# Paged decode inside a hybrid decoder step: value pages multiplied in runs of four, with ten page buffers and an 8 KB transfer scratch

## The chip, the cores and the metric

The kernel runs on one core of a Trainium2 chip. Its time is the device time of one execution in microseconds (us); the figure for a kernel is the median of several executions.

## The reference, cut to what matters

One inference step of a two-layer decoder: a gated-linear-attention (GLA) layer, then a differential-attention layer, each followed by a squared-ReLU MLP. There is a prompt of 1024 tokens (with 16 meta tokens before it), and eight running sequences that each get one new token. For those eight, the second layer attends over 4096 past tokens, held as 32 pages of 128 tokens in a pool:

```python
def diff_sample(x, cache_k, cache_v, page_table, w_in, lam, lam_init, g_sub, w_out):
    ...
    k_past = cache_k[page_table].reshape(B, past, DIFF_HEADS, 2, DIFF_DH)
    v_past = cache_v[page_table].reshape(B, past, DIFF_HEADS, DIFF_DV)
    k_all = jnp.concatenate([k_past, k], axis=1)
    v_all = jnp.concatenate([v_past, v], axis=1)
    o = diff_core(q, k_all, v_all, pos, jnp.arange(past + T), lam)

def diff_core(q, k, v, q_pos, k_pos, lam):
    s = jnp.einsum('bqhmd,bkhmd->bhmqk', q, k) * (DIFF_DH ** -0.5)
    p = jax.nn.softmax(jnp.where(mask, s, -jnp.inf), axis=-1)
    a = p[:, :, 0] - lam * p[:, :, 1]
    return jnp.einsum('bhqk,bkhe->bqhe', a, v)
```

A key page and a value page are each 128 x 1024 float32, 512 KB. Eight sequences of 32 pages make 256 key pages and 256 value pages, and each sequence has one more value row, that of its new token.

## The kernel before, in words

The large products (projections and MLPs of the prompt) run on TensorE as three float32r products of a split into a high and a low part (`mm3`, lines 185 to 188). The stages follow each other: GLA (up to some 520 us), then its output projection and the first MLP, then the projection of the second layer (`L1049` on), then prompt attention (from 1787 us), then its output projection and the second MLP.

The paged decode of the eight sequences is a generator, `decode()` (line 848), that runs beside the first MLP and the second layer's projection. Its step for sequence b handles, page by page, the keys of sequence b and the values of sequence b-1:

- `k_page` (line 783) loads a key page into a buffer of the pool `pgp` (line 726, `PGB` buffers of 4 KB per partition), multiplies it by the broadcast query (line 789, on VectorE, every fourth page on GpSimd) and sums it to scores (line 790, VectorE). Then its buffer is free.
- `v_load` (line 816) loads a value page into a buffer of the same pool. The buffer is held until TensorE has multiplied the page.
- `v_pages` (line 825) multiplies the value pages that are held: per page four products with 16 stationary columns each, in four column strips of the array, into one accumulator `acc` (line 830). They are plain float32, which the trace shows as two instructions each, so a page is eight matmul records.
- `soft` (line 792) is the softmax at the start of a sequence's values. Its transposes and sums pass through TensorE (lines 797, 801 and 806).
- `v_end` (line 836) takes the accumulator out after the 33rd value page (line 822 loads the new token's row).

All page loads are issued on SyncE's queue in `page` (lines 753 to 759). The sequences are numbered b = 0 to 8: b = 0 has keys alone, b = 8 values alone.

The order of instructions on each engine is fixed when the kernel is built, by a scheduler that plans with a timeline (`schedule_with_timeline_sim=True`). Page loads and key work stand in the background (`background()`, line 730): they have the lowest priority. The products of `v_pages` are not in the background; they stand at the priority of the place where the generator was advanced, ahead of most of the first MLP. The first product of a run is tied behind the reduction of a key page (`behind`, line 831), which fixes its place in the order:

```python
                    if len(held) == 2:
                        v_pages(held, w, acc, k)
                        held = []
                    held.append((n, v_load(b - 1, n)))
            if b > 0:
                held.append((NPG, v_load(b - 1, NPG)))
                v_pages(held, w, acc, None)
```

At the end of a sequence, and in b = 8, there is no such tie (`None`). The pages with numbers in `HOLD` (32 b + n from 212 to 227) are spread over the steps of the second layer's projection.

TensorE multiplies with the whole 128 x 128 array in `mm3`, and with strips of 16 columns in `v_pages`. A run here is a stretch of TensorE's order in which only products of line 830 follow each other.

GpSimd issues its own transfers (accumulating weight loads at line 1414, copies at lines 1149 to 1156 and 1378 to 1393). The scratch that the program reserves for such transfers is 16 KB per partition by default.

Of the kernel before, what the change touches and what calls it, by code (L numbers as in the profile page):

```python
# [32 lines left out]
EPS = 1e-5  # L33
NEG = -1e30
LAM_INIT = 0.8 - 0.6 * math.exp(-0.3)
PGB = 8
HOLD = range(212, 228)
HTB = 1
LEVELS = (64, 32, 16, 8, 4, 2, 1)
# [71 lines left out]
def hybrid_step(ctx, tc, A, dbg=None, upto=9):  # L111
    nc = tc.nc
# [19 lines left out]
    def smt():  # L132
        return sm.tile([P, 512], F32, name="smt")
# [591 lines left out]
    dp2 = de.enter_context(tc.tile_pool(name="dp2", bufs=2))  # L725
    pgp = de.enter_context(tc.tile_pool(name="pgp", bufs=PGB))
    bg_at = [10 ** 7]
# [46 lines left out]
    def k_start(b):  # L774
        sc = dp2.tile([P, NPG + 1, 16], F32, name="sc")
        qb = dp.tile([P, D], F32, name="qb")
        with background():
            dma(qb, A["qs"][b : b + 1, :].broadcast_to([P, D]))
            V.memset(sc[:, NPG, :], NEG)
            V.tensor_scalar(sc[:NS, NPG, :], own, other[:NS, b : b + 1], None, ALU.add)  # L780
        return sc, qb

    def k_page(b, n, sc, qb):
        with background():
            pg = page("cache_k", b, n)
            eng, after = (G, steps_g) if n % 4 == 3 else (V, steps_v)

            with tc.issue_after(after[-1]) if (b == 0 and n < 24 and after) or HOLD.start <= NPG * b + n < NPG * (HOLD.start // NPG + 1) else nullcontext():
                eng.tensor_tensor(pg, pg, qb, op=ALU.mult)  # L789
            return V.tensor_reduce(sc[:, n, :], pg.rearrange("p (h d) -> p h d", d=64), op=ALU.add, axis=AX.X).ins  # L790

    def soft(sc):

        mx = dp.tile([P, 16], F32, name="mx")
        V.tensor_reduce(mx, sc.rearrange("p n c -> p c n"), op=ALU.max, axis=AX.X)
        ps = smt()
        TE.transpose(ps[:16, :P], mx, ident)
        m1 = dp.tile([16, 1], F32, name="m1")
        V.tensor_reduce(m1, ps[:16, :P], op=ALU.max, axis=AX.X)
        ps = smt()  # L800
        TE.matmul(ps[:, :16], m1.broadcast_to([16, P]), ident[:16, :16], start=True, stop=True)
        V.tensor_tensor(sc, sc, bc(ps[:, :16], [P, NPG + 1, 16], 1), op=ALU.subtract)
        S.activation(sc, sc, AF.Exp, scale=0.125)
        V.tensor_reduce(mx, sc.rearrange("p n c -> p c n"), op=ALU.add, axis=AX.X)
        ps = smt()
        TE.matmul(ps[:, :16], one, mx, start=True, stop=True)
        cf = dp.tile([P, 16], F32, name="cf")
        V.reciprocal(cf, ps[:, :16])
        cv = cf.rearrange("p (c m) -> p c m", m=2)
        V.tensor_tensor(cv, cv, bc(lamv, [P, 8, 2], 1), op=ALU.mult)  # L810
        V.tensor_tensor(sc, sc, bc(cf, [P, NPG + 1, 16], 1), op=ALU.mult)
        av = sc.rearrange("p n (c m) -> p n c m", m=2)
        V.tensor_tensor(av[:, :, :, 0], av[:, :, :, 0], av[:, :, :, 1], op=ALU.add)
        return sc

    def v_load(b, n):
        with background():
            if n < NPG:
                return page("cache_v", b, n)
            pg = pgp.tile([P, D], F32, name="pg")  # L820
            G.memset(pg[:32], 0.0)
            dma(pg[:NS], A["v_rows_s"][0, :, 0].rearrange("b h d -> b (h d)"))
            return pg

    def v_pages(pages, w, acc, behind):

        for n, pg in pages:
            r = slice(0, P if n < NPG else 32)
            for i in range(4):
                m = TE.matmul(acc[i * TS : i * TS + 16, :256], w[r, n, :], pg[r, i * 256 : (i + 1) * 256], start=n == 0, stop=n == NPG).ins  # L830
                if behind is not None:

                    tc.add_manual_dep(m, behind.name, mybir.DependencyInfo(mybir.DependencyClass.NoSync, mybir.DependencyReason.DATA), reason="order")
                    behind = None

    def v_end(b, acc):

        ev = pgp.tile([P, D], F32, name="pg")[:, :256]
        G.memset(ev, 0.0)
        for i in range(4):  # L840
            S.copy(ev[i * TS : i * TS + 16, :], acc[i * TS : i * TS + 16, :256])
        pt = smt()
        for j in range(2):
            TE.transpose(pt[:, j * P : (j + 1) * P], ev[:, j * P : (j + 1) * P], ident)
        for j in range(2):
            V.tensor_copy(oT[:, j : 8 : 2, b], pt[:, 130 * j : 130 * j + 36 * 3 + 1 : 36])

    def decode():
        ks = None
        for b in range(NS + 1):  # L850
            prev = ks
            if b < NS:
                ks = k_start(b)
            if b > 0:
                w = soft(prev[0])
                acc = smt()
            held, k = [], None
            for n in range(NPG):
                if b == 0 or NPG * b + n in HOLD:
                    yield b  # L860
                if b < NS:
                    k = k_page(b, n, *ks)
                if b > 0:

                    if len(held) == 2:
                        v_pages(held, w, acc, k)
                        held = []
                    held.append((n, v_load(b - 1, n)))
# [3 lines that stand above are left out]
                v_end(b - 1, acc)  # L872
# [155 lines left out]
    for u in range(4):  # L1028
        dma(Yt[:, :, u * 256 : (u + 1) * 256], A["x_prompt"][0, :, u * 256 : (u + 1) * 256].rearrange("(t p) n -> p t n", p=P))
    stats = ln_stats(hp)  # L1030
    paged = decode()
    normalize(w_out(A["gla_w_out"][0], False, paged), stats, lambda c: to_fm(c, 0))
    normalize(mlp(paged), stats, lambda c: to_fm(c, 1))
# [538 lines left out]
```

## Time and profile before

| | |
|---|---|
| Median of 3 runs | 2902.23 us (2901.81 to 2903.02) |
| Profiled execution, its own time | 2897.76 us |
| Span of its trace | 2896.0 us |
| Granted TensorE clock, mean | 0.981 |
| TensorE busy | 2773.3 us (96%) |
| VectorE, ScalarE, GpSimd busy | 1882.9, 1043.5, 1132.4 us |
| Moved by DMA | 636.46 MB, mean 220 GB/s |

In the profile, PE is TensorE's matmul, PEld its weight load, DVE VectorE, ACT ScalarE, POOL GpSimd, SP SyncE; a q behind a name is the engine's queue of issues. L830 is line 830 of the kernel. A row of instructions has the start and the duration in us, the engine, the line, the operation, out<-in, the shapes and the count of merged records. Matmuls are pipelined and their ends are modelled, so the pace is read from their starts. A row of waits has who waited for whom, the total in us, how often, and the longest.

### The profile page before, as it was taken

The numbers are of one execution on the slowest core, as the hardware profiler recorded it, in microseconds if no ns is written. First come the engines' busy times: TensorE is split into PE (matmuls) and PEld (weight loads), VectorE is DVE, ScalarE is ACT, GpSimd is POOL, SyncE is SP. The second block draws the span as 40 slices with busy tenths as digits, with TensorE's granted clock in tenths as the row PEclk, the third lists the DMA queues.
The fourth block names the chain that finished last, engine by engine and source line by source line (L and its number), as shares of the span: only waits on it lengthen the run. The fifth ranks groups of instructions, "written<-read, shape, count | busy, mean of one in ns | idle before, by whom it ended". The sixth has DMA issues, their size and how long they took to land. (4 is left out here: it accounts for less than half of the span.)

```text
span 2896.0 us, 52075 instructions
## 1 busy us (share of the span) xinstructions
PE 2773.3 (96%) x19653; PEld 2267.4 (78%) x19653; DVE 1882.9 (65%) x2982; ACT 1043.5 (36%) x2075; POOL 1132.4 (39%) x867
## 2 busy tenths in 40 slices
PE   8889999999999999999999999989998999999997
PEld 5666767997777777777798988888988888797985
DVE  2565544567878777778768822888538846738378
ACT  3233444252221221221231112777424535345352
POOL 1231212234333433333333321122426766777664
PEclk9899999999999999999999998999999999999998
DMA  7557651624798898898668995463447678695894
GB/s 250 181 176 261 245 177 39 231 73 145 268 350 299 301 351 303 321 323 310 254 225 302 363 341 142 101 137 82 120 132 220 174 220 222 160 287 119 258 240 88
DMA packets 285366, 636.46 MB, mean 220 GB/s; under 512 B 25510, under 2 KB 141292, under 8 KB 273852
## 3 DMA queue, kind: packets, MB, share of 16 engines
q1 hardware_dynamic: 252716, 520.66, 52.4%
q0 software_dynamic: 32400, 112.50, 16.2%
q8 instruction: 154, 2.52, 0.4%
q14 instruction: 96, 0.79, 0.1%
HBM read 575.55 MB, written 44.06 MB: 214 GB/s over the span
## 5 line engine op out<-in xcount | busy, mean ns | idle before, releaser
L174 POOL TENSOR_TENSOR wlo<-raw,whi 128x512 fp32r<-128x512 f32 x256 | 357.1, 1408 | 730.1 <-ACT whi L173 635.8
L186 PE MATMUL mmt<-whi,XH 128*128 128x256 f32 (+1 forms) x1760 | 526.1, 300 | 2.2 <-ACT Y L310 2.0
L187 PE MATMUL mmt<-wlo,XH 128*128 128x256 f32 (+1 forms) x1760 | 525.9, 299 | 0.9 <-POOL wlo L174 0.9
L186 PE MATMUL mmt<-XH,whi 128*128 128x512 f32 (+1 forms) x1216 | 436.5, 360 | 7.0 <-DVE HL L183 6.6
L188 PE MATMUL mmt<-whi,XL 128*128 128x256 f32 x1536 | 436.6, 285 | 0.5 <-DVE XL L183 0.5
L188 PE MATMUL mmt<-XH,wlo 128*128 128x512 f32 (+1 forms) x1216 | 434.3, 358 | 0.0
L173 ACT CAST whi<-raw 128x512 fp32r<-128x512 f32 x256 | 153.1, 619 | 579.5 <-PE mmt L188 206.3
L187 PEld LDWEIGHTS mmt<-wlo,XH 128*128 128x128 f32 x1760 | 332.2, 189 | 30.9 <-issue 19.0
L186 PEld LDWEIGHTS mmt<-whi,XH 128*128 128x128 f32 x1760 | 331.5, 189 | 28.2 <-issue 13.5
L790 DVE TENSOR_REDUCE sc<-pg 128x16 f32<-128x1024 f32 x256 | 309.5, 1214 | 62.5 <-POOL pg L789 59.3
L187 PE MATMUL mmt<-XL,whi 128*128 128x512 f32 x768 | 307.3, 400 | 0.0
L188 PEld LDWEIGHTS mmt<-whi,XL 128*128 128x128 f32 x1536 | 289.8, 189 | 13.5 <-issue 11.8
L789 DVE TENSOR_TENSOR pg<-pg,qb 128x1024 f32<-128x1024 f32 x192 | 263.7, 1375 | 53.4 <-DMA pg<-in_cache_k 38.2
L789 POOL TENSOR_TENSOR pg<-pg,qb 128x1024 f32<-128x1024 f32 x64 | 158.8, 2482 | 297.9 <-DMA pg<-in_cache_k 182.4
L186 PEld LDWEIGHTS mmt<-XH,whi 128*128 128x128 f32 x1216 | 230.6, 190 | 54.8 <-issue 14.6
L188 PEld LDWEIGHTS mmt<-XH,wlo 128*128 128x128 f32 x1216 | 231.0, 190 | 38.1 <-issue 5.9
L187 PE MATMUL mmt<-wlo,HH 128*128 128x512 f32 x512 | 204.7, 400 | 0.0
L188 PE MATMUL mmt<-whi,HL 128*128 128x512 f32 x512 | 204.6, 400 | 0.0
L186 PE MATMUL mmt<-whi,HH 128*128 128x512 f32 x512 | 204.4, 399 | 0.0
L187 PEld LDWEIGHTS mmt<-XL,whi 128*128 128x128 f32 x768 | 145.5, 190 | 38.3 <-issue 7.1
L1416 POOL TENSOR_TENSOR wlo<-RW,whi 128x512 fp32r<-128x512 f32 x96 | 156.7, 1762 | 37.1 <-ACT whi L1415 37.1
L1416 POOL TENSOR_TENSOR wlo<-rw,whi 128x512 fp32r<-128x512 f32 x92 | 148.8, 1690 | 43.3 <-ACT whi L1415 43.2
(441 smaller groups left out, 5745.6 us busy)
## 6 DMA issues: line engine op xcount, KB each, us to landing
pg<-in_cache_k SPq DMA_DIRECT2D x256, 512.0 KB
pg<-in_cache_v SPq DMA_DIRECT2D x256, 512.0 KB
XH<-xc POOLq DMA_DIRECT2D x42, 1032.0 KB, 8.7
raw<-in_mlp_w SPq DMA_DIRECT2D x164, 256.0 KB
swt<-in_mlp_w SPq DMA_DIRECT2D x32, 1024.0 KB
rw<-in_mlp_w SPq DMA_DIRECT2D x116, 256.0 KB
RW<-in_mlp_w POOLq DMA_DIRECT2D x96, 256.0 KB, 6.1
xc<-XH POOLq DMA_DIRECT2D x14, 1032.0 KB, 7.6
```

The costliest lines, as they stand in the source:

```text
L173: S.copy(hi[:, c], raw)
L174: G.tensor_tensor(lo[:, c], raw, hi[:, c].bitcast(F32), op=ALU.subtract)
L186: TE.matmul(ps, ah, bh, start=first, stop=False)
L187: TE.matmul(ps, ah, bl, start=False, stop=False)
L188: TE.matmul(ps, al, bh, start=False, stop=last)
L789: eng.tensor_tensor(pg, pg, qb, op=ALU.mult)
L790: return V.tensor_reduce(sc[:, n, :], pg.rearrange("p (h d) -> p h d", d=64), op=ALU.add, axis=AX.X).ins
L1416: G.tensor_tensor(lo[:, k, :], t, hi[:, k, :].bitcast(F32), op=ALU.subtract)
```

## The change

Three numbers change. `v_pages` is called when four value pages are held, not two. The pool of page buffers has ten buffers, not eight. The scratch for GpSimd's transfers is 8 KB per partition, not 16; the two page buffers need 8 KB per partition.

```diff
-PGB = 8
+PGB = 10
+RUN = 4
...
-                    if len(held) == 2:
+                    if len(held) == RUN:
                         v_pages(held, w, acc, k)
                         held = []
...
-    nc = bacc.Bacc("TRN2", target_bir_lowering=False, num_devices=1)
+    nc = bacc.Bacc("TRN2", target_bir_lowering=False, num_devices=1, dynamic_dma_scratch_size=8192)
```

Per sequence, `v_pages` is called with fifteen groups of two pages and one of three before, and with seven groups of four and one of five after.

## The prediction

> **What bounds the kernel now.** I read the page first, then the busy time by stretches, the waits of TensorE, and the timeline around single runs of value pages.
>
> ```profile
> span 2896.0 us, 52075 instructions
> PE 2773.3 (96%) x19653; PEld 2267.4 (78%) x19653; DVE 1882.9 (65%) x2982; ACT 1043.5 (36%) x2075; POOL 1132.4 (39%) x867
> PE   8889999999999999999999999989998999999997
> DMA  7557651624798898898668995463447678695894
> ```
>
> TensorE is busy 96% of the span, and the slices from the eleventh to the twenty-fourth, where the pages are read, show it at nine tenths nearly throughout, with the DMA engines at six to nine tenths. Busy time of a pipelined engine proves little, so the next view cuts out the stretch from the first run of value pages to the end of the second layer's projection, and the third asks what TensorE waits for in it.
>
> ```profile
> core 0: us, PE busy (x) PEld busy (x) DVE busy (x) ACT busy (x) POOL busy (x), PEclk, DMA share, GB/s
> 520.00:766.00 246.00, 238.51 (x1404) 209.02 (x1402) 172.11 (x203) 74.00 (x122) 85.92 (x54) 0.98 0.51 169
> 766.00:1787.00 1021.00, 1019.55 (x7006) 795.71 (x7005) 703.18 (x831) 233.40 (x408) 348.67 (x222) 1.00 0.84 302
> ```
> ```profile
> PE smt L801 <- DVE m L799: 1.0, 1, 1.0
> PEld smt L830 <- DMA pg<-in_cache_v: 4.8, 13, 0.4
> ```
>
> In 1021 us TensorE is idle for 1.45 us, at full granted clock (1.00). The longest wait of its matmuls is one of 1.0 us, in a softmax; the weight loads of page products waited for a landing 13 times, 0.4 us at most, and these waits lie beside matmuls. DVE is busy 703 of 1021 us, the DMA engines 0.84 of the time. So this stretch is bound by TensorE's own sequence of instructions: a microsecond taken out of that sequence is a microsecond off the end, as long as pages, softmax and weights keep up.
>
> **What a run costs.** The timeline of TensorE around three runs of two, six and four pages (16, 48 and 32 records):
>
> ```profile
> 905.91 0.39 PE L187 MATMUL mmt<-wlo,HH 128*128 128x512 f32 x1
> 906.14 0.40 PE L188 MATMUL mmt<-whi,HL 128*128 128x512 f32 x1
> 906.46 1.06 PE L830 MATMUL smt<-pg,sc 128*16 128x256 f32 x16
> 907.45 0.50 PE L186 MATMUL mmt<-whi,HH 128*128 128x512 f32 x1
> 907.79 0.40 PE L187 MATMUL mmt<-wlo,HH 128*128 128x512 f32 x1
> ```
> ```profile
> 1010.45 0.40 PE L188 MATMUL mmt<-whi,HL 128*128 128x512 f32 x1
> 1010.78 2.78 PE L830 MATMUL smt<-pg,sc 128*16 128x256 f32 x48
> 1013.49 0.51 PE L186 MATMUL mmt<-whi,HH 128*128 128x512 f32 x1
> 1013.83 0.39 PE L187 MATMUL mmt<-wlo,HH 128*128 128x512 f32 x1
> ```
> ```profile
> 1562.95 0.28 PE L188 MATMUL mmt<-whi,XL 128*128 128x256 f32 x1
> 1563.16 1.92 PE L830 MATMUL smt<-pg,sc 128*16 128x256 f32 x32
> 1565.01 0.39 PE L186 MATMUL mmt<-whi,XH 128*128 128x256 f32 x1
> 1565.24 0.28 PE L187 MATMUL mmt<-wlo,XH 128*128 128x256 f32 x1
> 1565.36 0.28 PE L188 MATMUL mmt<-whi,XL 128*128 128x256 f32 x1
> ```
>
> The starts are what counts. Ordinary 512-column products start 0.23 us apart (905.91 to 906.14), 256-column ones 0.12 us (1565.24 to 1565.36). From the last ordinary product before a run to the second one after it there are two ordinary starts and the run: 907.79 - 906.14 = 1.65, less 2 x 0.23, leaves 1.19 us for two pages; 1013.83 - 1010.45 = 3.38, less 0.46, leaves 2.92 us for six; 1565.24 - 1562.95 = 2.29, less 0.24, leaves 2.05 us for four. From two to six pages that is 1.73 / 4 = 0.43 us a page, and what is left of a run, however long, is 1.19 - 2 x 0.43 = 0.33 us (2.05 - 4 x 0.43 = 0.33 for four pages). I use 0.32 us: the price of leaving the ordinary products and coming back. The change removes no page product; it removes such prices.
>
> [...]
>
> **How many prices go.** The products of line 830 in the whole trace, then the runs of one sequence (first two and last two of 13), then of the last sequence (two of its 27):
>
> ```profile
> L830 PE MATMUL smt<-pg,sc 128*16 128x256 f32 (+1 forms) x2112 | 139.0, 382 | 0.0
> ```
> ```profile
> 1133.15 2.78 PE L830 MATMUL smt<-pg,sc 128*16 128x256 f32 x48
> 1143.69 1.06 PE L830 MATMUL smt<-pg,sc 128*16 128x256 f32 x16
> ...
> 1215.35 1.06 PE L830 MATMUL smt<-pg,sc 128*16 128x256 f32 x16
> 1222.38 2.47 PE L830 MATMUL smt<-pg,sc 128*16 128x256 f32 x40
> ```
> ```profile
> 1697.00 0.62 PE L830 MATMUL smt<-pg,sc 128*16 128x256 f32 x8
> ...
> 1751.89 1.18 PE L830 MATMUL smt<-pg,sc 128*16 128x256 f32 x16
> ```
>
> 2112 records are 264 pages, eight sequences of 33. The sequence shown has six pages at once after its softmax, eleven runs of two, and five pages at its end: 13 runs out of 16 calls of `v_pages`, because the first three groups and the last two are ready together. Counted so on the timeline, the sequences b = 1 to 6 have 81 runs (13 or 14 each), b = 7 has 17 (three single pages at its end), and b = 8 has 27, nearly all single pages, because nothing ties them behind a key page: 125 runs in all, whose prices are 125 x 0.32 = 40 us. No merging can save more.
>
> After the change there are eight calls a sequence. At the start two groups of four may be ready together (one run fewer); at the end the group of five has no tie and may fall into two or three pieces (one or two more). I take 8 runs for b = 1 to 6 (48 for 81, 33 fewer), 9 for b = 7 (8 fewer), and 25 for b = 8, where ten buffers let more pages wait for the softmax (2 fewer): 43 fewer, 43 x 0.32 = 13.8 us. From below: if each end splits into three further pieces, 24 fewer, 7.7 us. From above: 7 runs in each of b = 1 to 7 and 22 in b = 8 make 71 runs, 54 fewer, 17.3 us. I take 13.8, since the sequence shown merges at both ends.
>
> **What the other parts cost.** Held pages. The loads wait for buffers already now:
>
> ```profile
> SPq L758 <- DVE sc L790: 102.4, 87, 4.0
> SPq L758 <- PE smt L830: 84.8, 73, 5.7
> ```
>
> SyncE's issues waited for a buffer from a key reduction 87 times and from a page product 73 times, and TensorE still had no idle time, so these waits are covered. Just before a run, two value pages and the key page under reduction hold three of eight buffers now, and four and one hold five of ten after: five are left for loads in both. A run will give back four at once instead of two, half as often. That cover is equal at its tightest, so I cost it at nothing; without it, a page takes 0.524 MB / 302 GB/s = 1.7 us to come in at this stretch's rate. In sequence b = 0 two more key pages can be fetched early: at most 2 x 1.7 = 3.5 us of transfer ahead of the weights, in a stretch (520 to 766 us) with the DMA engines at 0.51 and TensorE idle 7.5 us. Its bounds are a loss of 3.5 and a gain of 7.5 us; I take nothing, because with keys alone no page is held.
>
> What is late next, when TensorE gains 14 us? The last run ends near 1753 us and the accumulator is out soon after, while the projection goes on to 1787:
>
> ```profile
> 1757.08 0.23 DVE L846 COPY oT<-smt 128x4 f32<-128x4 f32 x2 [28.21 <-PE smt L844]
> 1787.18 0.27 PE L188 MATMUL mmt<-whi,XL 128*128 128x256 f32 x1
> ```
>
> That leaves 30 us, so the decode's own end doesn't take over.
>
> The scratch. GpSimd's transfers are those of q0:
>
> ```profile
> q0 software_dynamic: 32400, 112.50, 16.2%
> RW<-in_mlp_w POOLq DMA_DIRECT2D x96, 256.0 KB, 6.1
> ```
>
> None lies in the decode, and no row shows an issue that waits for scratch. I cost it at nothing; the other end is below. [...]
>
> The sum: 2897.8 us of the profiled execution (1.8 us around the span) less 13.8 makes 2884.0. The median of the runs is 4.5 us above the profiled execution, so the forecast is 2888.5 us, 0.47% faster.
>
> **The rivals.**
> *The pages come late (slower).* The first run after a softmax, and the first after each run of four, now need loads that could only be issued when four buffers came back at once. If the fixed order places runs closer behind the landings than now, TensorE stands still at line 830 with all ordinary products queued behind it, and ACT and DVE wait for those. If each of the 57 runs of b = 1 to 7 waits the 0.4 us that is the longest today, the loss is 22.8, net 9.0 us: 2911. The decisive point is 13.8 / 57 = 0.24 us a run. For it speaks that buffers are what loads wait for; against it, that five buffers are left in both cases.
> *The runs don't hold together (no change).* Only a run's first product is tied; in b = 8, without ties, nearly all pages stand alone. If groups of four fall into pairs, some 12 prices go, 3.8 us: 2898. Less than 18 fewer runs would be within 0.2%, which is 5.8 us and about what a measurement of this kernel can tell from no change.
> *GpSimd's issues stall on the smaller scratch (slower).* If one in ten of the 96 accumulating loads waited a landing of 6.1 us, 59 - 14 = 45 us: 2947. [...]
> *More than forecast.* All merges, 17.3 us, and the idle 7.5 us of the stretch before: 2877.
>
> **How the numbers follow.** The forecast has 0.60, more than that 0.07, no change 0.15, late pages 0.14, the scratch 0.04. So faster by over 0.2% has 0.67, within 0.2% 0.15, slower 0.18. The range goes from 2879, near the largest gain, to 2912, which takes in the late pages; it leaves out the scratch, worse delays and the last of the gain. The order is fixed anew for the whole program, so a few microseconds may move in stages that the change doesn't touch; they are inside this range.
>
> **What would show it.** Right: the timeline has runs of 32 records at 2.05 us from start to start, some 82 runs in place of 125, TensorE's idle time between the first run and the start of attention still under 3 us, and the first transpose of attention (now after 1787 us) some 14 us earlier, with the rest as long as before. Wrong: runs of 16 records as often as now; waits of line 830 for value pages of several microseconds in all on PE itself; waits at lines 797 to 806; or, after 1787 us, waits of GpSimd's issues at line 1414.

## The result, and the profile after

| | before | after |
|---|---|---|
| Median | 2902.02 us (20 executions, 2897.14 to 2908.79) | 2894.57 us (20 executions, 2888.45 to 2901.24) |
| Ratio, with its 95% interval | | 0.9978 [0.997, 0.9986] |
| Profiled execution, own time | 2897.76 us | 2895.22 us |

The changed kernel is 6.4 us faster by the ratio, 7.5 us by the medians. The forecast was 13.8 us. Note the last row: the two profiled executions are only 2.5 us apart, because that of before lies 4.3 us under its kernel's median and that of after 0.7 us above. A difference of this size can't be read from two spans; the traces say where time went within an execution, the medians how much.

In the changed file the lines stand one further down (page products at L831, ordinary products at L187 to L189). The head of its page:

```profile
span 2893.3 us, 52056 instructions
PE 2763.4 (96%) x19653; PEld 2275.0 (79%) x19653; DVE 1866.1 (64%) x2982; ACT 1046.3 (36%) x2075; POOL 1151.5 (40%) x867
PE   8889999999999999999999999889998999999997
DMA  7557741635798898888479975553447778695894
```

The number of matmul records is the same (19653), so no arithmetic has gone, and TensorE's busy time is 10 us less. The timeline around the first run after a softmax (two groups of four merged, 64 records), and around a run of four:

```profile
757.10 0.40 PE L187 MATMUL mmt<-XH,whi 128*128 128x512 f32 x1
757.42 3.65 PE L831 MATMUL smt<-pg,sc 128*16 128x256 f32 x64
761.00 0.50 PE L188 MATMUL mmt<-XL,whi 128*128 128x512 f32 x1
761.34 0.39 PE L189 MATMUL mmt<-XH,wlo 128*128 128x512 f32 x1
```
```profile
802.65 0.39 PE L189 MATMUL mmt<-whi,HL 128*128 128x512 f32 x1
802.97 1.92 PE L831 MATMUL smt<-pg,sc 128*16 128x256 f32 x32
804.82 0.50 PE L187 MATMUL mmt<-whi,HH 128*128 128x512 f32 x1
805.16 0.40 PE L188 MATMUL mmt<-wlo,HH 128*128 128x512 f32 x1
```

Read as in the prediction, four pages cost 805.16 - 802.65 - 0.46 = 2.05 us, and eight cost 761.34 - 757.10 - 0.46 = 3.78 us, which is 8 x 0.43 + 0.34. The stages by busy time, first of after (up to the first run, up to attention, attention, the rest), then the last two of before:

```profile
core 0: us, PE busy (x) PEld busy (x) DVE busy (x) ACT busy (x) POOL busy (x), PEclk, DMA share, GB/s
520.00:757.00 237.00, 230.36 (x1392) 202.14 (x1391) 172.74 (x209) 74.36 (x121) 85.77 (x54) 1.00 0.55 184
757.00:1777.60 1020.60, 1015.91 (x7044) 808.24 (x7042) 687.44 (x829) 236.97 (x414) 369.73 (x224) 1.00 0.83 300
1777.60:2075.30 297.70, 267.62 (x1881) 240.77 (x1880) 235.24 (x726) 199.71 (x464) 68.15 (x81) 0.93 0.49 113
2075.30:2893.00 817.70, 774.90 (x4910) 671.01 (x4908) 516.41 (x677) 334.53 (x605) 514.84 (x435) 0.98 0.70 192
```
```profile
1787.00:2077.00 290.00, 265.39 (x1885) 238.65 (x1885) 230.28 (x728) 199.12 (x465) 68.12 (x81) 0.94 0.51 117
2077.00:2896.00 819.00, 774.87 (x4908) 669.38 (x4906) 520.64 (x675) 333.53 (x605) 516.53 (x435) 0.98 0.71 191
```

Attention starts at 1777.6 us, where it started at 1787; then it lasts 297.7 us, where it lasted 290.0. The decode is shorter, and most of what it gained in these two executions is gone by the end of a stage whose instructions the change doesn't touch. (The stretch from the first run to attention is as long as before, 1020.6 us against 1021, because the first run stands earlier; from 520 us on, the way to attention is 1257.6 us long, where it was 1267.) TensorE's waits between the first run and attention, and SyncE's for buffers, in after:

```profile
PE mmt L187 <- DVE Y L1015: 2.2, 2, 1.3
PE smt L802 <- DVE m L800: 1.2, 1, 1.2
PE smt L807 <- DVE mx L805: 0.9, 1, 0.9
PE axt L950 <- DVE XL L184: 0.4, 1, 0.4
```
```profile
SPq L759 <- DVE sc L791: 98.2, 75, 4.0
SPq L759 <- PE smt L831: 46.6, 72, 4.6
```

No matmul waits for a page; the weight loads of page products waited for a value page 7 times, 0.4 us at most. The loads wait for a buffer almost as often as before (147 times, it was 160), and less long (144.8 us, it was 187.2).

### The profile page after: what moved, and what is told of

The parts are those of the page before. It is cut to its first block, busy times and chain, and to the rows that moved or that the text cites. A ratio compares the mean times of both kernels' runs of the same rounds, so it can differ in the third digit from the quotient of the medians.

```text
span 2893.3 us, 52056 instructions
## 1 busy us (share of the span) xinstructions
PE 2763.4 (96%) x19653; PEld 2275.0 (79%) x19653; DVE 1866.1 (64%) x2982; ACT 1046.3 (36%) x2075; POOL 1151.5 (40%) x867
## 4 chain that ended last, share of the span: by engine, by line
PE 70%; DVE 11%; DMA 10%; issue 5%; POOL 3%; ACT 1%; SPq 0%; DVEq 0%; POOLq 0%; ACTq 0%
PE mmt L187 17%; PE mmt L188 16%; PE mmt L189 16%; PE smt L831 4%; PE axt L187 2%; PE axt L188 2%; PE axt L189 2%; PE smt L1203 2%; DMA XH<-xc 2%; DMA rw<-in_mlp_w 1%; DMA swt<-in_mlp_w 1%; DVE Y L1490 1%; PE axt L1198 1%; PE smt L507 1%; DMA pg<-in_cache_k 1%
## 5 line engine op out<-in xcount | busy, mean ns | idle before, releaser
L175 POOL TENSOR_TENSOR wlo<-raw,whi 128x512 fp32r<-128x512 f32 x256 | 371.7, 1465 | 755.5 <-ACT whi L174 675.0
L187 PE MATMUL mmt<-whi,XH 128*128 128x256 f32 (+1 forms) x1760 | 524.3, 300 | 3.6 <-ACT Y L311 2.0
L187 PE MATMUL mmt<-XH,whi 128*128 128x512 f32 (+1 forms) x1216 | 437.1, 360 | 4.0 <-DVE HL L184 3.6
L189 PE MATMUL mmt<-whi,XL 128*128 128x256 f32 x1536 | 435.4, 285 | 0.0
L189 PE MATMUL mmt<-XH,wlo 128*128 128x512 f32 (+1 forms) x1216 | 433.0, 357 | 0.0
L187 PEld LDWEIGHTS mmt<-whi,XH 128*128 128x128 f32 x1760 | 330.9, 189 | 28.0 <-issue 11.8
L189 PEld LDWEIGHTS mmt<-whi,XL 128*128 128x128 f32 x1536 | 289.5, 189 | 11.1 <-issue 10.1
L187 PEld LDWEIGHTS mmt<-XH,whi 128*128 128x128 f32 x1216 | 230.9, 190 | 52.3 <-issue 13.7
L790 POOL TENSOR_TENSOR pg<-pg,qb 128x1024 f32<-128x1024 f32 x64 | 165.0, 2580 | 250.1 <-DMA pg<-in_cache_k 179.3
L189 PEld LDWEIGHTS mmt<-XH,wlo 128*128 128x128 f32 x1216 | 230.8, 190 | 34.7 <-issue 2.1
L187 PE MATMUL mmt<-whi,HH 128*128 128x512 f32 x512 | 204.7, 401 | 4.5 <-DVE Y L1015 4.4
L189 PE MATMUL mmt<-whi,HL 128*128 128x512 f32 x512 | 203.9, 398 | 0.0
```

What stands on the lines that cost most here:

```text
L175: G.tensor_tensor(lo[:, c], raw, hi[:, c].bitcast(F32), op=ALU.subtract)
L187: TE.matmul(ps, ah, bh, start=first, stop=False)
L189: TE.matmul(ps, al, bh, start=False, stop=last)
```

## The experiments

The numbers of runs below are counted in the order of TensorE's instructions: 125 in the kernel before, 86 in the changed one. A price is what one run costs beside its pages, 0.32 us. "TensorE's order in attention" is the order of its instructions from the first transpose of attention on: the planner gives one in the kernel before, and another in the changed kernel.

**One part at a time.** From the changed kernel, the spread pages alone are moved (e1); or the runs are put back to two, the ten buffers kept (e2); or the eight buffers and the 16 KB are put back, the runs of four kept (e4). From the kernel before, the scratch alone is cut (e3).

```
e1:  -HOLD = range(212, 228)        +HOLD = range(216, 232)
e2:  -RUN = 4                       +RUN = 2
e4:  -PGB = 10                      +PGB = 8        (and the default scratch)
e3:  -num_devices=1)                +num_devices=1, dynamic_dma_scratch_size=8192)
```

> The changed kernel with the held pages four later (numbers 216 to 231 spread over the projection instead of 212 to 227). Its decode keeps runs of four (83 runs of value pages in the built order, 86 in the changed kernel, 125 before), and its built order of TensorE in prompt attention is the one of the kernel before, instruction by instruction, not the one of the changed kernel. Theory A (the decode gives back 0.32 us per run, and the other order in attention takes some of it away): the stretch from 766 us to the first transpose of attention shrinks by about 13 us, attention lasts 288 to 290 us as before instead of 297, and the whole is about 13 us faster than before, ratio 0.9955. Theory B (the smaller scratch slows attention): attention 297 as in the changed kernel, ratio 0.9975. Theory C (attention scatters from execution to execution, whatever its order): no tie between order and duration.

> The changed kernel with runs of two (ten buffers, 8 KB of scratch). 118 runs of value pages in the built order; its built order of TensorE in attention is exactly that of the changed kernel. Theory A: 7 runs fewer than before give 2 us, attention takes 5 to 8 us more than before, so 3 to 6 us slower than before, ratio 1.001 to 1.002. Theory B: the same sign, for another reason. Theory C: 2 us faster, ratio 0.999.

> The kernel before with the scratch of 8 KB alone. The built orders are those of before. Theory A and C: no change, ratio 0.9995 to 1.0005, attention 288 to 290 us. Theory B: some 5 to 8 us slower, ratio 1.002, all of it in attention, and longer times from issue to landing of GpSimd's transfers.

> The kernel before with runs of four and eight buffers (16 KB of scratch): 96 runs of value pages in the built order. Theory of the prediction (0.32 us per run, five or more buffers left are enough): with four held pages and a key page only three of eight buffers are left for loads, so this is the tight case. If buffers are no bound, the stretch up to attention shrinks by 29 x 0.32 = 9 us. If they are, waits of line 831 for value pages appear on PE and the gain is under 5 us. Attention has a third order here, whose duration theory A doesn't foretell.

| | runs | median | ratio to before |
|---|---|---|---|
| e1 | 83 | 2890.51 us | 0.9963 [0.9951, 0.9974] |
| e2 | 118 | 2913.52 us | 1.0032 [1.0014, 1.005] |
| e3 | 125 | 2902.09 us | 1.0003 [0.999, 1.0016] |
| e4 | 96 | 2939.21 us | 1.0139 [1.0116, 1.0161] |

e3: no cost of the smaller scratch shows, to some 4 us. e2: the buffers by themselves are no gift; with them and runs of two the kernel is 9 us slower than before, more than the 3 to 6 expected. e4: runs of four without more buffers lose 40 us. Just before a run only three of the eight buffers are left for loads, and the wait that the prediction feared as its first rival is there, with the idle time around it:

```profile
PE smt L831 <- DMA pg<-in_cache_v: 10.1, 9, 2.2
PE mmt L187 <- DVE Y L1015: 7.4, 8, 3.3
PE smt L802 <- DVE m L800: 5.2, 1, 5.2
```
```profile
766.00:1828.60 1062.60, 1024.96 (x7008) 808.31 (x7007) 683.33 (x828) 232.22 (x408) 352.85 (x222) 0.99 0.83 290
```

From the first run to attention it takes 1062.6 us, with 37.6 us of idle time, where before had 1021 and 1.45. Waits for value pages are 10.1 us of these 37.6; most of the others are waits of the first MLP, the softmax and the projection for VectorE, and why these grew wasn't tried by itself.

Two expectations on attention failed here. In e1 and e3 it was to last 288 to 290 us, since their order in attention is that of before; it lasted 297.1 and 294.4 us. So its length doesn't follow the order alone. What else it follows is taken up below.

**More buffers, and longer runs.** Eleven buffers with 4 KB of scratch and runs of four (e5) or five (e6); the two known kernels again on the same chip (e7, e8).

```
e5:  -PGB = 10                      +PGB = 11
     -dynamic_dma_scratch_size=8192 +dynamic_dma_scratch_size=4096
e6:  the same, and  -RUN = 4        +RUN = 5
```

> Runs of four with eleven buffers and 4 KB of scratch: 79 runs of value pages in the built order, and TensorE's built order in attention is again that of the kernel before. If 0.32 us a run is right and six buffers left are as good as five, the stretch from the end of the first layer to attention shrinks by 46 x 0.32 = 14.7 us against the kernel before (12.5 in the changed kernel). Theory A (the changed kernel's other order in attention costs some 4 us): about 14 us faster than before, ratio 0.995. Theory C (attention's length follows the clock and not the order; the changed kernel's loss lies elsewhere): the stretch gains the same, the whole gains about 5 us less, as in the changed kernel, ratio 0.997.

> Runs of five with eleven buffers (five left for loads just before a run, as before and in the changed kernel) and 4 KB of scratch: 63 runs. By 0.32 us a run the stretch shrinks by 62 x 0.32 = 19.8 us. Rival: the price was no price of a run but of something else that fell with eight to ten buffers; then it shrinks by 12 to 13 us as in the changed kernel. Attention has an order of its own here.

> The kernel before, unchanged, for a second profile. Theory A: attention lasts 288 to 292 us again (289.3 in its first profile). Theory C: it scatters, 288 to 298 us, and its length goes with the time at half clock in it (34 us in the first profile); the stretch before it, 1271 us, and the rest stay within 2 us.

> The changed kernel, unchanged, for a second profile. Theory A: attention lasts 296 to 299 us again (297.5 in its first profile). Theory C: it scatters, 288 to 298 us; the stretch before it is 1259 us within 2 us in both theories.

| | runs | median | ratio to before |
|---|---|---|---|
| e5 | 79 | 2913.59 us | 1.0042 [1.0025, 1.0058] |
| e6 | 63 | 2903.47 us | 1.0009 [0.9996, 1.0022] |
| e7 (before) | 125 | 2901.99 us | 1.0001 [0.9988, 1.0014] |
| e8 (after) | 86 | 2895.33 us | 0.9967 [0.9953, 0.9981] |

e5 and e6 are clear misses: fewer prices, and no gain. The waits of TensorE in e5, from the end of GLA to attention:

```profile
PE mmt L187 <- DVE HL L184: 10.9, 6, 4.2
PE mmt L187 <- DVE Y L1015: 6.5, 5, 2.9
PE mmt L188 <- POOL wlo L175: 4.5, 3, 2.8
PE axt L950 <- ACT Y L939: 3.0, 2, 2.4
```

None is for a page. They are waits of the first MLP and of the normalization for VectorE, GpSimd and ScalarE, and TensorE is idle 28.8 us between GLA and attention (22.3 in e6, 8.9 before). An eleventh buffer has room for one more key page, and the key work is done on VectorE and GpSimd, for which TensorE waits 17.4 and 4.5 us in these rows. That the key work is what they are late by is read from these rows and was not tried by itself. The scratch of 4 KB was not run by itself either, but it can hardly be the cause: in the traces of before and after, as in e5's, GpSimd issues no transfer between 300 us and the start of attention, and the time is lost there (attention starts at 1797.4 us).

e7 and e8 repeat the two orders of attention: it lasted 290.7 us in e7 and 298.7 us in e8, as expected if the length goes with the order. The stretch ahead of it scattered by more than the 2 us expected: attention started 3.0 us earlier in e7 than in the first profile of before, and 2.6 us later in e8 than in the first of after.

**The kernel cut before attention.** To see what the decode gains without the noise of what follows, the kernel before, the changed one, and e2 were ended where attention would start. These kernels leave out attention, the last projection and the second MLP, and with them the loads for these stages that would be issued early.

```
     if upto == 3:
+        de.close()
         return dbg(locals())
...
-        hybrid_step(tc, A)
+        hybrid_step(tc, A, lambda v: None, 3)
```

> The kernel before, ended where prompt attention would start (1787.4 us in its trace): attention, the last projection and the second MLP are left out. Alone it says little; it is the base of the next two. From the traces I expect about 1795 us (1787 us, some us at the end, and the scatter of the clock).

> The changed kernel, ended at the same place; 86 runs of value pages, as in the whole kernel. Theory D (the decode gains what its trace shows, and some of it is given back from attention on, by another order there and more time at half clock): 39 prices of 0.32 us less 1 to 2 us of idle time make it 10 to 12.5 us shorter than the cut kernel before. Rival S (the decode itself gains no more than the whole kernel, the rest was the scatter of single profiles): 6 to 8 us shorter. The middle is 9 us.

> Ten buffers and 8 KB of scratch with runs of two, ended at the same place; 118 runs. Theory D: 7 prices fewer (-2.2 us) and about 5.5 us of idle time and other delay, 2 to 4 us longer than the cut kernel before, since the rest of the whole kernel's 9 to 11 us lies from attention on. Rival S: all of it lies ahead of attention, 8 to 11 us longer. If ten buffers cost nothing, as the prediction had it: 2 us shorter.

With them, runs of five with ten buffers:

```
e12: -RUN = 4                       +RUN = 5
     -HOLD = range(212, 228)        +HOLD = range(208, 224)
```

> Runs of five with ten buffers, and the spread pages 208 to 223, so that TensorE's order in attention is that of the kernel before: 68 runs, and four buffers left for loads just before a run. Theory D with four buffers being enough: 57 prices fewer (-18.2 us), 2 to 4 us given back in the decode: 2886 to 2888, ratio 0.995. If four left is already short (three left cost 38 us in the decode, five left 1 to 2), TensorE waits for value pages at line 831 for 5 us or more: 2893 or worse.

| | runs | median | ratio to the whole kernel before |
|---|---|---|---|
| e9, before, cut | 125 | 1789.91 us | 0.617 [0.6159, 0.618] |
| e10, after, cut | 86 | 1778.82 us | 0.6129 [0.6119, 0.614] |
| e11, ten buffers and runs of two, cut | 118 | 1790.83 us | 0.6166 [0.6152, 0.6179] |
| e12, whole | 68 | 2898.53 us | 0.9988 [0.9976, 1.0001] |

Up to attention the change brings 11.1 us by the medians and 11.9 by the ratios, of the 39 x 0.32 = 12.5 that the runs are worth, to some 3 us. So the cut decode gains nearly all that its prices say, which speaks for theory D: most of the rest of the loss lies from attention on. In e11 it is between 0.9 us longer (medians) and 1.2 us shorter (ratios), less than the 2 to 4 us longer that theory D expected; 7 runs fewer are worth 2.2, so the buffers cost the cut decode 1 to 3 us, not the 9 of e2.

The traces of the whole kernels put more of the loss ahead of attention. It starts at 1787.4, 1784.4 and 1784.8 us in three profiles of the order of before (before, e7, e3), and at 1777.7, 1780.3 and 1780.6 us in three of the changed kernel (after, e8, e14): 6 us earlier in the mean, not 11. In e2's profile it starts at 1792.3 us, later than in any of the first three. Single executions scatter by as much (the five of e10 by 6.3 us), so how the loss is split at the start of attention is known to a few microseconds only.

e12 gains 3.5 us where 57 prices are 18.2. Its waits from the first run to attention, and the same stretch by busy time:

```profile
PE mmt L187 <- DVE Y L1015: 3.1, 3, 1.2
PE smt L802 <- DVE m L800: 3.0, 2, 2.3
PE axt L950 <- ACT Y L939: 2.5, 2, 1.9
PE mmt L187 <- DVE HL L184: 2.1, 2, 1.3
```
```profile
751.20:1778.50 1027.30, 1016.19 (x7042) 813.96 (x7041) 709.30 (x828) 236.83 (x413) 363.74 (x224) 1.00 0.83 298
```

The expected sign of a shortage, a wait at line 831, isn't there; 11.1 us of idle time are, spread over waits for VectorE and ScalarE. That may be part of the missing 14.7 us. The rest stays open: its profiled execution (2890.16 us) is 8 us shorter than its median.

**What is given back from attention on.** First the two orders side by side, e1's kernel (e13) and the changed one (e14), with the cut of e1's (e15).

> The changed kernel with the spread pages 216 to 231: 83 runs, TensorE's order from attention on that of the kernel before. If the order in attention is what gives back 4 us: 42 prices, 13.4 us, less 1 to 2 us in the decode: 11.5 to 12.5 us faster than before, ratio 0.996. If all kernels with ten buffers lose alike from attention on: 8 us faster, ratio 0.9973.

> The changed kernel: 7 us faster than before, ratio 0.9976. If the order in attention is the cause, 4 to 5 us slower than e13; if not, within 1.5 us of it (three runs more are 1 us).

> The kernel of e13, ended where attention would start; attention, the last projection and the second MLP are left out. 83 runs: 42 prices less 1 to 2 us below the cut kernel before, 1777 to 1779 us, 1 us below the cut changed kernel, by either theory. What e13 gains less than this cut is given back from attention on.

Then the kernel before, with nothing but its spread pages moved: to 215, where the planner gives it the changed kernel's order in attention on TensorE, VectorE and ScalarE (e16, and e18 cut before attention), and to 218, where it keeps its own (e17).

```
e16: -HOLD = range(212, 228)        +HOLD = range(215, 231)
e17: -HOLD = range(212, 228)        +HOLD = range(218, 234)
```

> The kernel before (eight buffers, runs of two, 16 KB) with the spread pages 215 to 230: 123 runs of value pages, and from attention on the changed kernel's order. If that order by itself costs 4 to 6 us: 2905 to 2907 us, 3.5 to 5.5 us slower than before (2 runs fewer give 0.6 us). If the order costs nothing without ten buffers: 2901 to 2902 us.

> The kernel before with the spread pages 218 to 233: 122 runs, from attention on its own order. 3 runs fewer, 1 us: 2901 us by either theory. It guards against moved pages costing time by themselves.

> The kernel of e16, ended where attention would start; attention, the last projection and the second MLP are left out. 123 runs, no more than 1 us from the cut kernel before: 1789 to 1790 us by either theory. What e16 loses more than this lies from attention on.

| | runs | order in attention | median | ratio to the whole kernel before |
|---|---|---|---|---|
| e13 | 83 | of before | 2889.02 us | 0.9947 [0.9929, 0.9965] |
| e14 (after) | 86 | of after | 2896.41 us | 0.9982 [0.9966, 0.9998] |
| e15, e13 cut | 83 | | 1777.48 us | 0.6123 [0.611, 0.6135] |
| e16 | 123 | of after | 2911.23 us | 1.0025 [1.0012, 1.0037] |
| e17 | 122 | of before | 2907.79 us | 1.0013 [0.9998, 1.0028] |
| e18, e16 cut | 123 | | 1796.76 us | 0.6191 [0.6178, 0.6203] |

Put together, in us against the kernel before, by the ratios times 2902 (where a kernel was timed more than once, their mean). By the intervals above, the first column is known to some 3 to 4 us, the second to 2 to 5, and the difference to some 4 to 6:

| kernel | up to attention | whole | difference: from attention on |
|---|---|---|---|
| after (first result, e8, e14; e10) | -11.9 | -7.0 | +4.9 |
| e1 and e13 (order of before; e15) | -13.6 | -13.1 | +0.5 |
| e2 (order of after; e11) | -1.2 | +9.3 | +10.5 |
| e16 (before, order of after; e18) | +6.1 | +7.3 | +1.2 |

With ten buffers the kernel in the order of before keeps its gain, and the two in the other order lose 5 and 10 us: that half of e13's theory held, and e14 is 7.4 us slower than e13, where 4 to 5 were expected. e16 was to show the order costing 4 to 6 us by itself. It is 7 us slower than before, a little more than forecast, but for another reason: 6 us of it are lost up to attention, where e18 was to be unchanged. Moving the spread pages is itself not free; e17, expected at 2901 us, points the same way, though its interval takes in no change. From attention on e16 loses 1 us, give or take 4, which neither shows nor excludes the order's cost.

The profiles say more. The transposes of the scores (L1197, in the changed file L1198) wait for VectorE; the two rows of this wait, in before, e13 and e17 (order of before), then in after, e14 and e16 (order of after):

```profile
PE axt L1197 <- DVE as L1188: 4.8, 5, 2.0
PE axt L1197 <- DVE ast L1186: 2.6, 4, 1.2
```
```profile
PE axt L1198 <- DVE ast L1187: 7.0, 5, 3.1
PE axt L1198 <- DVE as L1189: 2.4, 3, 1.9
```
```profile
PE axt L1197 <- DVE as L1188: 3.8, 4, 1.9
PE axt L1197 <- DVE ast L1186: 3.5, 3, 2.5
```
```profile
PE axt L1198 <- DVE as L1189: 7.1, 5, 3.5
PE axt L1198 <- DVE ast L1187: 3.5, 2, 3.2
```
```profile
PE axt L1198 <- DVE as L1189: 8.8, 7, 3.5
PE axt L1198 <- DVE ast L1187: 0.3, 1, 0.3
```
```profile
PE axt L1197 <- DVE as L1188: 8.6, 6, 3.5
PE axt L1197 <- DVE ast L1186: 0.3, 1, 0.3
```

In the changed kernel's order the wait for the last combination of the scores (as) is longer, 7.1 to 8.8 us against 2.4 to 4.8, with eight buffers as with ten. But both rows are waits of the same line's transposes for VectorE, and they have to be taken together: they are 7.4, 9.4 and 7.3 us in the order of before and 10.6, 9.1 and 8.9 in the other, so the waits at this line account for 1 or 2 us. Attention by busy time in e17 and e13, then in e14 and e16:

```profile
1790.60:2084.20 293.60, 267.56 (x1878) 240.91 (x1878) 229.97 (x726) 199.30 (x464) 68.12 (x81) 0.93 0.50 115
```
```profile
1774.40:2071.60 297.20, 269.04 (x1880) 242.14 (x1879) 231.72 (x726) 199.69 (x464) 68.14 (x81) 0.93 0.49 113
```
```profile
1780.60:2074.50 293.90, 265.20 (x1878) 237.69 (x1878) 233.91 (x726) 199.49 (x464) 68.15 (x81) 0.94 0.50 115
```
```profile
1798.00:2095.10 297.10, 265.39 (x1878) 238.99 (x1878) 233.41 (x726) 199.35 (x464) 68.25 (x81) 0.94 0.50 113
```

At a granted clock of 0.94 attention takes 290.0 us in before and 293.9 and 297.1 in the other order; at 0.93, 293.6 and 297.2 in the order of before and 297.7 in after. So the clock matters beside the order. Summed over the trace's records of the clock, attention ran at half clock for 34.1 us in before and e14, 37.5 in e7 and e16, 41.0 in after, e2, e3, e12 and e17, and 44.4 in e1, e5, e8 and e13. (e5 and e12 have the order of before, e2 and e8 that of after.) Compared at equal time at half clock, attention in the changed kernel's order is 4.6 us longer at 34.1 (293.9 against 289.3), 6.5 at 37.5 (297.2 against 290.7), 2.3 to 4.6 at 41.0 (297.5 and 298.2 against 293.6 to 295.2) and 1.5 to 1.8 at 44.4 (298.7 against 296.9 to 297.2): some 4 us.

The idle time says the same. In the rows above TensorE is busy for 265 to 269 us in either order; it is idle for 26.0 us in e17 and 28.2 in e13, but 28.7 in e14 and 31.7 in e16. Before has 24.6 and after 30.1. Over all profiles of the two orders the idle time is 24.4 to 28.2 us in eight of the order of before, and 28.7 to 31.7 in five of the other: the two don't overlap, and their means are 3.3 us apart. In e16 this order came with eight buffers and runs of two. So the order itself makes attention 3 to 4 us longer. The waits at the transposes are only part of it; where the rest of the idle time comes from is open.

The changed kernel doesn't run at a lower clock on the whole. The records have only full and half clock (1.0 and 0.5 in before and after), so an execution's time at half clock is 2 x (1 - mean clock) x span. Averaged over the executions, and less that of the cut kernels, it is 77 us from attention on in before and 78 in after, a difference that is known to some 6 us. At a clock of 0.5 that is an estimated 1 us of the loss, to some 3.

e1's kernel is faster than before and after: 0.9963 and 0.9947 of before.

## Why the prediction was right, and wrong

*The price of a run: right.* 2.05 us for four pages in both traces, 3.78 for eight. The cut kernels agree without a trace: 39 prices of 0.32 us are 12.5, and 11.1 to 11.9 us were measured up to attention, to some 3.

*The number of runs: slightly off.* 86 instead of 82, 1.3 us of the sum. A typical sequence is now 8, 4, 4, 4, 4, 6, 1, 1, 1 pages: the beginning merged as assumed, and the end splits into up to three single pages. b = 1 to 6 have 50 runs (48 assumed) and b = 7 has 8 (9 assumed). Most of the miss is b = 8: it has 28 runs, one more than before, where ten buffers were to let pages merge into 25. In the working, the sum from below doesn't come out: three further pieces at each of seven ends leave 43 - 21 = 22 runs fewer, 7.0 us, not 24 and 7.7; the forecast doesn't rest on it.

*Held pages and ten buffers: right on the cover, not on the price.* No matmul waits for a page in after, and e4, with three buffers left, shows what the rival looks like when its condition is met: 40 us lost in all. That five left are enough was the right reading of the buffers. But their cost, put at nothing, was not nothing: about 1 us in the cut decode (12.5 against 11.1 to 11.9), 1 to 3 in e11, and more by the traces of the whole kernel. TensorE's idle time from the first run to attention is 4.7 us in after, 6.7 in e8 and 8.8 in e14, over the 3 us that were set as the mark; it was 1.4 in before. The longest of these waits is one in a softmax (line 802: 1.2, 3.3 and 5.2 us), a sign that the prediction had named. Counted from 516 us on, the idle time is 11.3, 12.3 and 14.2 us against 8.9 in before, so the cost is 1 to 5 us. Whether the buffers or the longer runs make it was not separated. The early key pages cost nothing between GLA and the first run (idle 6.6 us, it was 7.5).

*The scratch: right.* e3's ratio is 1.0003. The accumulating loads (RW) take a median of 6.1 us from issue to landing in before and in after alike.

*"The rest as long as before": the step that failed.* The prediction put what lies after 1787 us at zero and let "a few microseconds" of it into the range alone. But the change gave attention another order on TensorE, and of the terms put at nothing this is the one that the runs show most clearly: 3 to 4 us more in attention, by five profiles of the new order against eight of the old, and 4 to 5 us, to some 4, as the difference between cut and whole kernels. The other is the price of the held pages and ten buffers, above. The sum then reads 13.8 less 1.3 (runs), less 1 to 5 (buffers and longer runs), less 3 to 4 (attention), which makes 3.5 to 8.5; 6.4 to 7.5 was measured. The trace of before could have warned of it: attention was its stage with the lowest granted clock (0.94) and 24.6 us of idle time, and the order there is fixed by the same planner that a moved decode disturbs. It could not have given the sign.

*The rivals.* Late pages did not come, nor did the scratch stall. The runs hold together except at the ends of the sequences and in b = 8.

## What to carry to other kernels

Price the change between two kinds of matmul from start to start, with runs of three lengths; here it was the same, 0.33 to 0.34 us, for two, four, six and eight pages. But a planner that orders the whole program turns a local edit into another order far behind it, so a gain of half a per cent needs the kernel cut behind the edited stage, timed beside the whole one, to see what the stage earned and what was lost later. A mere tie elsewhere (here the place of the spread pages) can be worth nearly as much as the edit: in the changed kernel it restored the old order and took another 6 us off (e1, e13). It is no free gift: in the kernel before, moving the same pages cost 7 us (e16).

## What was not expected of the hardware

More buffers went with a slower kernel: 1.0042 with eleven (and 4 KB of scratch) at 79 runs, against 0.9978 with ten at 86. And single executions differ in the clock: in the traces of before and after the stretches at half clock last 3.4 us or a multiple of it, up to 23.9 (but for the last of each, 15.9 and 18.4 us, with which the records end), and attention with one and the same order on TensorE took 289.3 us with 34.1 us at half clock (before), 294.4 with 41.0 (e3) and 297.1 with 44.4 (e1). At the 0.5 of the records 10.3 us more at half clock would cost an estimated 5.2 us; 7.8 were measured between the first and the last of these, and what makes up the difference isn't shown.
